# Block 1's expert sums on the matrix engine, gathers 25 places back, and a norm gain as columns

## The chip, the cores and the metric

The kernel runs on one core of a Trainium2 chip. The metric is the device time of one launch in microseconds, median of three runs. The engines are named as in the profile: PE multiplies matrices (its weight loads are listed apart as PEld), DVE is the vector engine, ACT the scalar engine, POOL issues the gathers (indirect DMAs), SP issues all other DMAs. Every engine, and each of the two DMA issuers, takes its instructions in the order that was fixed when the kernel was compiled.

## The reference, cut to what matters

One decoder layer over 1024 tokens of width 1024, all in fp32:

```python
h = x
h = h + hybrid_mixer(rms_norm(h, norm_mix), ...)          # convolution + delta rule, w_in, w_out
h = h + memory_cross_attention(rms_norm(h, norm_x), ...)  # 256 memory tokens, w_xq, w_xo
xn = rms_norm(h, norm_ffn)
# PEER: per token 8 heads x 16 best of 128*128 product keys = 128 experts
q = xn @ w_query; idx, gates = top16 of the sums of two top16 lists, softmax
act = gelu(einsum("td,ted->te", xn, expert_u[idx]))       # 128 dot products per token
y   = einsum("te,ted->td", gates * act, expert_v[idx])    # sum of 128 rows per token
out = rms_norm(h + y, norm_final)
```

`expert_u` and `expert_v` have 16384 rows of 1024. `rms_norm(h, norm_ffn)` is h times one number per token, times a gain per channel.

## The kernel before, in words

The tokens are eight blocks of 128. Three chunks go through mixer, attention and routing: `ca` (blocks 0, 1), `cb` (blocks 2 to 5, "the middle pass") and `cc` (blocks 6, 7).

The experts are done in two ways. Blocks 2 to 5 are done **densely**: `densify` builds on DVE, PE and ACT a table of gates per expert (`gd`), and `dense` multiplies these 512 tokens with all 16384 rows of both tables. Blocks 0, 1, 6 and 7 are **gathered**: for each of the 128 slots, POOL gathers one row of `expert_u` per token (a tile `g` of 512 KB, six buffers), and DVE forms the dot products in one instruction per slot (`gather_u`, L948). Then one row of `expert_v` per token is gathered. The sum over slots is made in one of two ways, by a bit of the constant `VD` for each block:

- `gather_v` with the bit set: one DVE instruction per slot adds gate times row to `y` (L1033);
- `gather_p` with the bit clear: the gathers run by token instead of by slot, the gates are spread out by DVE (L970), and PE makes four products for each pair of gathers (L984) in one PSUM bank `acc`. After 64 tokens ACT copies the bank (L996) to a short tile `t_s` (four buffers, also used by the routing), and SP takes it through DRAM (`yd`).

`VD` = 194 has bits 1, 6 and 7 set: only block 0 goes over PE. Both ways end in `finish`, which takes `g` buffers for h, for the final gain and, after `gather_p`, for y.

The order is written by hand. `merge` interleaves generators in proportion to their weights, and each `yield` is one step. `gathers(0)` has 518 steps: 3 of routing, 131 of `gather_u(0)` (with block 1's routing), 256 of `gather_u(1)` alternating with `gather_v(0)`, 128 of `gather_v(1)`. G1 to G4 = 98, 90, 107 and 17 of them stand beside the middle pass's projection, recurrence, attention and routing, G5 = 120 beside `tables2` (routing and `densify` of blocks 2 to 5) and the chunk `cc`; what is left stands beside `dense`, ahead of `gathers(6)`. `at` gives the steps of a generator another priority than their place: PG1 = 100 puts the first 295 steps (beside the middle pass) 100 places ahead, PG2 = -25 puts those beside G4 and G5 25 places behind. The tile scheduler then fixes the order of each engine by these priorities and its own estimate of when operands are ready.

`queries` normalises a chunk, writes the rows to DRAM (`xnd`) for `gather_u` and `dense`, and turns them to channels (`to_channels`). The gain `g_ffn` is applied to the rows there (L801), from a row that SP loads into all partitions (L796).

Of the kernel before, what the change touches and what calls it, by code (L numbers as in the profile page):

```python
# [9 lines left out]
F32 = mybir.dt.float32  # L10
# [6 lines left out]
OP = mybir.AluOpType  # L17
# [3 lines left out]
P = 128  # L21
SEQ = 1024
D = 1024
# [16 lines left out]
CSTART = [sum(CAND[:r]) for r in range(16)]  # L40
NCAND = sum(CAND)
NSLIP, CLOSE, PACE = 4, 3, 517
G1, G2, G3, G4, G5 = 98, 90, 107, 17, 120
A5 = -1
C4, T5 = 61, 92
NSHORT, NRAW, NHI, NLO, NG, LU, LV, VD = 6, 4, 2, 4, 6, 1, 1, 194
PG1, PG2, PG3, PT, PR, PD = 100, -25, 0, 0, 0, 0


def constants():  # L50
# [26 lines left out]
def merge(*gens):  # L77

    done = [0] * len(gens)
    live = [True] * len(gens)  # L80
    while any(live):
        j = min((i for i in range(len(gens)) if live[i]), key=lambda i: done[i] / gens[i][1])
        try:
            yield next(gens[j][0])
            done[j] += 1
        except StopIteration:
            live[j] = False


def run(*gens):  # L90
    for g in gens:
        for _ in g:
            pass
# [7 lines left out]
def steps(gen, n):  # L101
    for _ in range(n):
        if next(gen, 0) == 0:
            return
        yield
# [7 lines left out]
def _body(ctx, tc, I, out, dbg, front_only):  # L113
    nc = tc.nc
    act = nc.scalar.activation
    stt = nc.vector.scalar_tensor_tensor
    tt = nc.vector.tensor_tensor
    tsc = nc.vector.tensor_scalar
# [6 lines left out]
    gp = ctx.enter_context(tc.tile_pool(name="gp", bufs=NG))  # L125
# [3 lines left out]
    def dbgout(name, ap, idx):  # L129
        if name in dbg:  # L130
            nc.sync.dma_start(dbg[name][idx], ap)


    def unit():
        return qp.tile([P, 4, T], F32, name="unit")
# [9 lines left out]
    def psum():  # L145
        banks["n"] += 1
        return pp.tile([P, T], F32, name="ps" if banks["n"] % 2 or not banks["both"] else "po")
# [5 lines left out]
    def rows(n):  # L153

        r = []
        for _ in range((n + 1) // 2):
            v = unit().rearrange("p a t -> p (a t)")
            r += [v[:, 0:D], v[:, D:2 * D]]
        return r[:n]
# [29 lines left out]
    g_mix, g_x, g_mem, g_ffn = (cols[:, 8 * i:8 * i + 8] for i in range(4))  # L189
# [79 lines left out]
    def normalise(blocks):  # L269
        ss = sp.tile([P, NB], F32, name="ssn")  # L270
        rstd = sp.tile([P, NB], F32, name="rstdn")
        n = len(blocks)
        for b in range(n):
            sumsq(ss[:, b:b + 1], blocks[b])
        rsqrt(rstd[:, :n], ss[:, :n], 1.0 / D, EPS)
        return rstd
# [11 lines left out]
    def split_parts(nt=T):  # L288

        def one():  # L290
            if nt == T:
                return Parts([unit().bitcast(F32R) for _ in range(2)], 4)
            v = unit().bitcast(F32R).rearrange("p a t -> p (a t)")[:, :KD * nt]
            return Parts([v.rearrange("p (k t) -> p k t", k=KD)], KD)

        return one(), one()

    def to_channels(xhi, xlo, blocks, gain):

        nt = len(blocks) * P  # L300
        for k in range(KD):
            ps = psum()
            for b, x in enumerate(blocks):
                nc.tensor.transpose(ps[:, b * P:(b + 1) * P], x[:, k * P:(k + 1) * P], ident)
            if gain is None:
                act(xhi[:, k, :nt], ps[:, :nt], AF.Copy)
                tt(xlo[:, k, :nt], ps[:, :nt], xhi[:, k, :nt].bitcast(F32), op=OP.subtract)
            else:
                act(xhi[:, k, :nt], ps[:, :nt], AF.Copy, scale=gain[:, k:k + 1])
                stt(xlo[:, k, :nt], ps[:, :nt], gain[:, k:k + 1], xhi[:, k, :nt].bitcast(F32),  # L310
                    op0=OP.mult, op1=OP.subtract)

    def proj_ct(src, x, nt, key=None):

        xhi, xlo = x
        ps = psum()
        hi, lo = load_w(src, key)
        for k in range(KD):
            js = slice(k * P, (k + 1) * P)
            mm3(ps[:, :nt], hi[:, js], lo[:, js], xhi[:, k, :nt], xlo[:, k, :nt], k == 0, k == KD - 1)  # L320
            if k % 4 == 3:
                yield
        return ps[:, :nt]
# [466 lines left out]
    def queries(c):  # L790

        t0, NB, T = c.t0, c.nb, c.T
        hv = c.h
        rstd = normalise(hv)
        gffn = unit().rearrange("p a t -> p (a t)")[:, :D]
        nc.sync.dma_start(gffn, I["g_ffn_row"].partition_broadcast(P))  # L796
        xs = rows(NB)
        for b in range(NB):
            tb = slice(t0 + b * P, t0 + (b + 1) * P)
            nc.sync.dma_start(hd2[tb], hv[b])  # L800
            stt(xs[b], hv[b], rstd[:, b:b + 1], gffn, op0=OP.mult, op1=OP.mult)  # L801
            nc.sync.dma_start(xnd[tb], xs[b])
            dbgout("xn", xs[b], tb)
        x = split_parts(T)
        to_channels(x[0], x[1], xs, None)
        yield
        for b in range(NB):
            routes[c.b0 + b] = Route(c.b0 + b)
        for hh in range(4):
            pair = []  # L810
            keys = sp.tile([P, 2, P], F32, name="keys")
            nc.sync.dma_start(keys, I["keysT"][:, 2 * hh:2 * hh + 2])
            for i in (2 * hh, 2 * hh + 1):
                ps = yield from proj_ct(I["w_pq"][i], x, T, (c.keep, "w_pq", i))
                pair.append(short()[:, :T])
                act(pair[-1], ps, AF.Copy)
                yield
            for b in range(0, NB, 2):
                yield from best_keys(c.b0 + b, hh, pair, keys, b * P)
# [118 lines left out]
    def gather_u(r):  # L938

        tb = r.tb  # L940
        xn = gp.tile([P, D], F32, name="xn", bufs=1)
        nc.sync.dma_start(xn, xnd[tb * P:(tb + 1) * P])
        idx = r.a = gp.tile([P, NSLOT], F32, name="g_a", bufs=2)
        stt(idx, r.ki, 128.0, r.kj, op0=OP.mult, op1=OP.add)
        ii = r.ii = gp.tile([P, NSLOT], I32, name="g_ii", bufs=2)
        nc.vector.tensor_copy(ii, idx)
        for k, g in gathered("expert_u", ii, LU):
            stt(g, g, 1.0, xn, op0=OP.mult, op1=OP.mult, accum_out=r.a[:, k:k + 1])  # L948
            yield
# [131 lines left out]
    def dense(first):  # L1081

        xs = rows(NB)
        for b in range(NB):
            nc.sync.dma_start(xs[b], xnd[first + b * P:first + (b + 1) * P])
        x = split_parts()
        to_channels(x[0], x[1], xs, None)
        ev = I["expert_v"].rearrange("(i j) d -> j i d", j=P)
        y = []

# [50 lines left out]
        for b in range(NB):  # L1141
            tb = slice(first + b * P, first + (b + 1) * P)
# [69 lines left out]
    ga = at(pg, gathers(0))  # L1212
    tables2 = at("PT", tables(2))
# [5 lines left out]
    qb = queries(cb)  # L1219
    next(qb)  # L1220
    rest = at("PR", chain(inproj(cc), recurrence(cc), outproj(cc), cross(cc), queries(cc)))
    run(merge((steps(ga, G4), G4), (qb, 32), (steps(rest, C4), C4)))
    run(merge((steps(ga, G5), G5), (tables2, T5), (rest, 195 - C4)))

    pg['now'] = 'PG3'
    run(merge((chain(ga, at('PG3', gathers(6))), 1036 - G1 - G2 - G3 - G4 - G5), (at("PD", dense(2 * P)), PACE)))
# [52 lines left out]
```

## Time and profile before

| | |
|---|---|
| median of three runs | 3265.38 us (3265.27 to 3266.77) |
| the profiled execution | 3260.8 us, of which 3259.0 us is the span |
| PE, DVE, ACT, POOL busy | 86%, 78%, 41%, 40% of the span |
| mean granted TensorE clock | 0.913 of 2.4 GHz |
| DMA | 984.74 MB, 302 GB/s over the span |
| gathered | 1024 tiles of 512 KB: 536.94 MB |

In a row of a group of instructions, "busy, mean ns" is the time in which at least one of them ran and the mean of one; "idle before" is the time in which the engine stood still just ahead of them, with what ended most of it. In a row of stretches the columns are busy time and number of instructions of each engine, then the granted clock, the share of the DMA engines' time in use, and GB/s.

### The profile page before, as it was taken

The numbers are of one execution on the slowest core, as the hardware profiler recorded it, in microseconds if no ns is written. First come the engines' busy times: TensorE is split into PE (matmuls) and PEld (weight loads), VectorE is DVE, ScalarE is ACT, GpSimd is POOL, SyncE is SP. The second block draws the span as 40 slices with busy tenths as digits, with TensorE's granted clock in tenths as the row PEclk, the third lists the DMA queues.
The fourth block names the chain that finished last, engine by engine and source line by source line (L and its number), as shares of the span: only waits on it lengthen the run. The fifth ranks groups of instructions, "written<-read, shape, count | busy, mean of one in ns | idle before, by whom it ended". The sixth has DMA issues, their size and how long they took to land.

```text
span 3259.0 us, 42839 instructions
## 1 busy us (share of the span) xinstructions
PE 2786.7 (86%) x14826; PEld 2309.3 (71%) x14826; DVE 2550.9 (78%) x5311; ACT 1349.8 (41%) x2463; POOL 1319.0 (40%) x1028
## 2 busy tenths in 40 slices
PE   7897699847788898475665799999999999999997
PEld 7886588745554687364644687888888888888885
DVE  6654898797544588998887999887888888888874
ACT  5444343312222353334433354445444444454444
POOL 0000024475544332402453246555555655555530
PEclk9998789968989799687877899999999999999998
DMA  7555759898988998616999689999999999999983
GB/s 282 189 176 203 271 209 368 290 331 312 359 311 319 365 368 324 242 78 238 370 345 377 233 289 344 372 345 326 349 345 347 345 342 347 341 336 345 346 304 104
DMA packets 351417, 984.74 MB, mean 302 GB/s; under 512 B 30304, under 2 KB 99552, under 8 KB 347104
## 3 DMA queue, kind: packets, MB, share of 16 engines
q0 software_dynamic: 147456, 536.94, 44.9%
q1 hardware_dynamic: 203744, 445.08, 37.8%
q8 instruction: 116, 1.90, 0.2%
q14 instruction: 101, 0.83, 0.1%
HBM read 901.68 MB, written 80.22 MB: 301 GB/s over the span
## 4 chain that ended last, share of the span: by engine, by line
PE 44%; DVE 10%; DMA 3%; issue 2%; ACT 1%; POOL 0%; SPq 0%; DVEq 0%; ACTq 0%; POOLq 0%
PE ps L259 7%; PE ps L261 7%; PE ps L260 7%; PE po L261 7%; PE po L260 7%; PE po L259 7%; DVE unit L1066 1%; DVE g_y L1033 1%; DMA g<-expert_u,g_ii 1%; PE ps L1072 1%; DVE unit L1063 1%; DVE unit L1064 1%; DMA g<-expert_v,g_ii 1%; DMA wraw<-w_pq 1%; DMA unit<-g_ffn_row 1%
## 5 line engine op out<-in xcount | busy, mean ns | idle before, releaser
L931 POOL DMA_INDIRECT g<-expert_u,g_ii x512 | 636.7, 1244 | 1032.3 <-DVE t_s L833 443.5
L246 ACT ACTIVATE whi<-wraw 128x1024 fp32r<-128x1024 f32 x452 | 480.0, 1062 | 868.0 <-PE ps L260 481.7
L931 POOL DMA_INDIRECT g<-expert_v,g_ii x384 | 549.7, 1432 | 642.5 <-DVE g_y L1033 338.9
L948 DVE SCALAR_TENSOR_TENSOR g<-g,xn 128x1024 f32<-128x1024 f32 x512 | 618.0, 1218 | 165.0 <-DMA g<-expert_u,g_ii 155.7
L259 PE MATMUL ps<-unit,whi 128*128 128x512 f32 (+1 forms) x1784 | 655.5, 368 | 16.2 <-ACT whi L246 7.6
L261 PE MATMUL ps<-unit,wlo 128*128 128x512 f32 (+1 forms) x1784 | 648.5, 364 | 7.6 <-DMA wlo<-lod 4.9
L260 PE MATMUL ps<-unit,whi 128*128 128x512 f32 (+1 forms) x1784 | 649.1, 364 | 0.0
L252 DVE TENSOR_TENSOR wlo<-wraw,whi 128x1024 fp32r<-128x1024 f32 x332 | 406.4, 1225 | 293.5 <-ACT whi L246 284.9
L1033 DVE SCALAR_TENSOR_TENSOR g_y<-g,g_a,g_y 128x1024 f32<-128x1024 f32 x381 | 487.7, 1280 | 16.8 <-DMA g<-expert_v,g_ii 13.3
L260 PE MATMUL po<-wlo,unit 128*128 128x512 f32 x1136 | 442.8, 390 | 0.0
L261 PE MATMUL po<-whi,unit 128*128 128x512 f32 x1136 | 442.4, 389 | 0.0
L259 PEld LDWEIGHTS ps<-unit,whi 128*128 128x128 f32 x1784 | 348.8, 196 | 79.3 <-issue 11.5
L261 PEld LDWEIGHTS ps<-unit,wlo 128*128 128x128 f32 x1784 | 348.1, 195 | 60.0 <-DMA wlo<-lod 5.1
L259 PE MATMUL po<-whi,unit 128*128 128x512 f32 x1136 | 382.8, 391 | 1.9 <-ACT whi L246 1.9
L260 PEld LDWEIGHTS ps<-unit,whi 128*128 128x128 f32 x1784 | 348.8, 196 | 49.4 <-DVE unit L310 0.8
L259 PEld LDWEIGHTS po<-whi,unit 128*128 128x128 f32 x1136 | 213.2, 188 | 49.9 <-ACT whi L246 3.6
L260 PEld LDWEIGHTS po<-wlo,unit 128*128 128x128 f32 x1136 | 213.3, 188 | 46.6 <-issue 1.9
L261 PEld LDWEIGHTS po<-whi,unit 128*128 128x128 f32 x1136 | 213.4, 188 | 45.2 <-issue 0.8
L1126 ACT ACTIVATE unit<-po 128x512 f32<-128x512 f32 x256 | 152.7, 597 | 144.7 <-PE po L261 136.8
L977 POOL DMA_INDIRECT g<-expert_v,g_y x128 | 132.3, 1034 | 156.8 <-DVE g L948 53.3
L1113 ACT ACTIVATE po<-unit 128x512 f32<-128x512 f32 x248 | 144.4, 605 | 0.0
L1072 PE MATMUL ps<-unit 128*128 128x128 f16 x1024 | 86.6, 239 | 59.6 <-DVE unit L1066 47.7
(391 smaller groups left out, 4080.3 us busy)
## 6 DMA issues: line engine op xcount, KB each, us to landing
wraw<-u_t SPq DMA_DIRECT2D x128, 512.0 KB
wraw<-expert_v SPq DMA_DIRECT2D x128, 512.0 KB
wlo<-lod SPq DMA_DIRECT2D x120, 512.0 KB
wraw<-w_in SPq DMA_DIRECT2D x84, 512.0 KB
gd<-unit SPq DMA_DIRECT2D x32, 1024.0 KB
unit<-gd SPq DMA_DIRECT2D x32, 1024.0 KB
lod<-wlo SPq DMA_DIRECT2D x60, 512.0 KB
wraw<-w_out SPq DMA_DIRECT2D x24, 512.0 KB
```

Of the source, the lines that this page charges most:

```text
L246: act(hi, raw, AF.Copy)
L252: tt(lo, raw, hi.bitcast(F32), op=OP.subtract)
L259: nc.tensor.matmul(ps, lh, rh, start=first, stop=False, skip_group_check=open_)
L260: nc.tensor.matmul(ps, lh, rl, start=False, stop=False, skip_group_check=open_)
L261: nc.tensor.matmul(ps, ll, rh, start=False, stop=last, skip_group_check=open_)
L931: nc.gpsimd.indirect_dma_start(out=g, out_offset=None, in_=I[table], in_offset=bass.IndirectOffsetOnAxis(ap=ii[:, k:k + 1], axis=0))
L948: stt(g, g, 1.0, xn, op0=OP.mult, op1=OP.mult, accum_out=r.a[:, k:k + 1])
L977: nc.gpsimd.indirect_dma_start(out=g, out_offset=None, in_=I["expert_v"], in_offset=bass.IndirectOffsetOnAxis(ap=iT[:, t:t + 1], axis=0))
L1033: stt(y, g, a[:, k:k + 1], y, op0=OP.mult, op1=OP.add)
L1072: nc.tensor.matmul(ps[:, u * P:(u + 1) * P], part[i][:, g, :, t], oj[:, g, :, t], start=i == 0, stop=i == 1)
L1113: act(pss[b], y[b][:, half * 512:(half + 1) * 512], AF.Copy)
L1126: act(y[b][:, half * 512:(half + 1) * 512], pss[b], AF.Copy)
```

## The change

- `VD` becomes 192: block 1 goes through `gather_p` instead of the DVE sum.
- G5 becomes 206, and the weight of those steps 1.25 x 206: all 518 steps of `gathers(0)` now stand beside `tables2` and `cc` or earlier, and the last 206 are spread over the first four fifths of that stretch. Beside `dense` only `gathers(6)` is left.
- PG1 becomes -25: the gathers beside the middle pass stand 25 places behind their place instead of 100 ahead.
- `queries` no longer multiplies by the gain row and no longer loads it; `to_channels` applies the gain as a column per channel, in `queries` and in `dense`. The rows in `xnd` lack the gain, so `gather_u` loads the gain row into a `g` buffer for each block and multiplies `xn` by it.

```diff
-G1, G2, G3, G4, G5 = 98, 90, 107, 17, 120
+G1, G2, G3, G4, G5 = 98, 90, 107, 17, 206
-NSHORT, NRAW, NHI, NLO, NG, LU, LV, VD = 6, 4, 2, 4, 6, 1, 1, 194
-PG1, PG2, PG3, PT, PR, PD = 100, -25, 0, 0, 0, 0
+NSHORT, NRAW, NHI, NLO, NG, LU, LV, VD = 6, 4, 2, 4, 6, 1, 1, 192
+PG1, PG2, PG3, PT, PR, PD = -25, -25, 0, 0, 0, 0
@@ queries
-        gffn = unit().rearrange("p a t -> p (a t)")[:, :D]
-        nc.sync.dma_start(gffn, I["g_ffn_row"].partition_broadcast(P))
...
-            stt(xs[b], hv[b], rstd[:, b:b + 1], gffn, op0=OP.mult, op1=OP.mult)
+            tsc(xs[b], hv[b], rstd[:, b:b + 1], None, op0=OP.mult)
...
-        to_channels(x[0], x[1], xs, None)
+        to_channels(x[0], x[1], xs, g_ffn)
@@ gather_u
+        gffn = gp.tile([P, D], F32, name="g")
+        nc.sync.dma_start(gffn, I["g_ffn_row"].partition_broadcast(P))
+        tt(xn, xn, gffn, op=OP.mult)
@@ dense
-        to_channels(x[0], x[1], xs, None)
+        to_channels(x[0], x[1], xs, g_ffn)
@@ the order
-    run(merge((steps(ga, G5), G5), (tables2, T5), (rest, 195 - C4)))
+    run(merge((steps(ga, G5), 1.25 * G5), (tables2, T5), (rest, 195 - C4)))
```

## Rows read from the trace of the kernel before

**Rows 1.** The page: busy time of each engine, with its share of the span.

```profile
PE 2786.7 (86%) x14826; PEld 2309.3 (71%) x14826; DVE 2550.9 (78%) x5311; ACT 1349.8 (41%) x2463; POOL 1319.0 (40%) x1028
```

**Rows 2.** Busy time by stretch: length, PE, PEld, DVE, ACT, POOL, clock, DMA, GB/s.

```profile
444.00:600.00 156.00, 155.21 (x703) 128.94 (x702) 125.63 (x252) 71.58 (x127) 72.92 (x60) 0.97 0.97 370
600.00:800.00 200.00, 122.47 (x832) 105.70 (x832) 173.82 (x346) 45.10 (x123) 119.82 (x107) 0.79 0.86 303
800.00:1100.00 300.00, 246.27 (x1179) 166.43 (x1177) 152.59 (x338) 78.15 (x153) 139.60 (x134) 0.90 0.90 339
...
1300.00:1380.00 80.00, 40.65 (x283) 26.70 (x283) 72.80 (x192) 28.52 (x71) 34.27 (x27) 0.69 0.70 251
1380.00:1500.00 120.00, 72.03 (x615) 65.53 (x615) 112.72 (x335) 42.75 (x112) 0.23 (x1) 0.81 0.21 80
1500.00:1700.00 200.00, 133.59 (x954) 111.46 (x954) 180.35 (x293) 85.83 (x233) 104.28 (x66) 0.80 0.93 354
1700.00:1840.00 140.00, 84.89 (x573) 71.47 (x574) 116.60 (x377) 43.19 (x94) 38.61 (x29) 0.73 0.85 324
...
2000.00:3200.00 1200.00, 1197.69 (x5279) 989.85 (x5278) 988.41 (x1145) 575.59 (x832) 675.10 (x489) 1.00 0.94 339
```

**Rows 3.** L1033 alone by stretch: DVE busy, clock, DMA, GB/s.

```profile
1300.00:1500.00 200.00, 0.00 (x0) 0.76 0.41 148
1500.00:1840.00 340.00, 117.80 (x92) 0.77 0.90 342
1840.00:2000.00 160.00, 44.56 (x35) 0.99 0.86 294
```

**Rows 4.** Groups of instructions between 1300 and 1840 us.

```profile
L931 POOL DMA_INDIRECT g<-expert_v,g_ii x98 | 149.5, 1525 | 326.8 <-ACT unit L1076 120.5 <-DVE g_y L1033 105.8 <-DVE t_s L832 25.9
L1033 DVE SCALAR_TENSOR_TENSOR g_y<-g,g_a,g_y 128x1024 f32<-128x1024 f32 x92 | 117.8, 1280 | 10.5 <-DMA g<-expert_v,g_ii 9.3 <-issue 0.2
L1072 PE MATMUL ps<-unit 128*128 128x128 f16 x1024 | 86.6, 239 | 59.6 <-DVE unit L1066 47.7 <-ACT unit L1076 4.6 <-DVE unit L310 1.4
```

**Rows 5.** The chain of waits, 1300 to 1840 us: shares by line, one piece.

```profile
by line: DVE unit L1066 7.5%; issue 6.9%; DVE g_y L1033 5.9%; PE ps L1072 4.9%; DVE unit L1063 4.8%; DVE unit L1064 4.0%; PE ps L259 3.9%; DMA g<-expert_v,g_ii 3.8%; DMA wraw<-w_pq 3.5%; DMA unit<-g_ffn_row 3.5%; PE ps L260 3.4%; PE ps L261
...
1735.71 18.73 DMA unit<-g_ffn_row
```

**Rows 6.** Block 0's products: two PE groups, a weight-load group, 1300 to 1380 us.

```profile
L984 PE MATMUL ps<-g,g_y 128*32 128x512 f32 x256 | 42.1, 711 | 11.8 <-DMA g<-expert_v,g_y 11.8
L984 PE MATMUL po<-g,g_y 128*32 128x512 f32 x256 | 37.8, 665 | 24.8 <-DMA g<-expert_v,g_y 23.8 <-issue 0.9
L984 PEld LDWEIGHTS po<-g,g_y 128*32 128x32 f32 x256 | 5.2, 111 | 35.0 <-DMA g<-expert_v,g_y 19.8 <-DVE g L948 8.5 <-issue 6.2
L984 PE MATMUL ps<-g,g_y 128*32 128x512 f32 x64 | 12.4, 855 | 6.6 <-DMA g<-expert_v,g_y 6.6
```

**Rows 7.** PE in order of time: start, us, and the idle time before in brackets.

```profile
410.49 0.48 PE L304 MATMUL po<-call,unit 128*128 128x128 f32 x1 [23.83 <-DVE unit L421]
...
719.33 0.47 PE L695 MATMUL ps<-call,unit 128*128 128x128 f32 x1 [25.90 <-ACT unit L691]
```

**Rows 8.** DVE in order of time at 711 us, in the same columns.

```profile
710.95 1.23 DVE L948 SCALAR_TENSOR_TENSOR g<-g,xn 128x1024 f32<-128x1024 f32 x1 [1.22 <-DMA g<-expert_u,g_ii]
...
712.10 0.15 DVE L234 TENSOR_TENSOR rs_t<-rs_y 128x4 f32<-128x4 f32 x1
```

**Rows 9.** Who waited for whom: us in total, times, longest.

```profile
DVE g L948 <- DMA g<-expert_u,g_ii: 155.7, 73, 8.8
...
POOL g L931 <- ACT unit L1076: 120.5, 1, 120.5
```

**Rows 10.** Groups of instructions over the whole span.

```profile
L801 DVE SCALAR_TENSOR_TENSOR unit<-unit,rstdn 128x1024 f32<-128x1024 f32 x8 | 9.8, 1281 | 16.6 <-DMA unit<-g_ffn_row 16.5
...
L970 DVE TENSOR_TENSOR g_y<-g_y,masks 128x256 f32<-128x256 f32 x16 | 6.6, 416 | 2.0 <-PE po L984 1.1 <-ACT g_y L963 0.5 <-PE ps L984 0.4
...
L718 DVE TENSOR_SCALAR unit<-unit,rstdn 128x1024 f32<-128x1024 f32 x8 | 5.7, 769 | 0.1
```

More of the change, by code (lines that the diff above doesn't have):

```diff
@@ L800, in queries @@
             nc.sync.dma_start(hd2[tb], hv[b])
-            stt(xs[b], hv[b], rstd[:, b:b + 1], gffn, op0=OP.mult, op1=OP.mult)
+            tsc(xs[b], hv[b], rstd[:, b:b + 1], None, op0=OP.mult)
             nc.sync.dma_start(xnd[tb], xs[b])
-            dbgout("xn", xs[b], tb)
         x = split_parts(T)
-        to_channels(x[0], x[1], xs, None)
+        to_channels(x[0], x[1], xs, g_ffn)
         yield
```

## Prediction

> **What bounds the kernel now.** I read the page first, then a table of stretches, then the groups and the chain of waits in the stretch that the change touches most. PE is busy 86% of the span, DVE 78% [rows 1], but that is a mean over two regimes. From 2000 to 3200 us PE is busy 1197.69 of 1200 us at the full 2.4 GHz [rows 2]: this is the dense part. Its matmuls are not touched, so whatever leaves it (gathers, DVE sums) is worth nothing there; it only begins earlier or later. The kernel's time is therefore the moment at which the dense part has all it needs, near 1840 us, plus a fixed 1420 us.
>
> Before that PE has holes. In 600 to 800 us it is busy 122 of 200 us, in 800 to 1100 us 246 of 300, and from 1300 to 1840 us 331 of 540 (40.65 + 72.03 + 133.59 + 84.89), at a clock between 0.69 and 0.81 [rows 2]. DVE is the full engine where PE is empty: 174 of 200 us in 600 to 800, and 72.8 + 112.7 + 180.4 + 116.6 = 482 of the 540 us [rows 2]. DMA moves 339 to 370 GB/s in three of these stretches and only 80 GB/s from 1380 to 1500 us [rows 2]: there one wait of 120.5 us keeps POOL from gathering [rows 9]. So no engine is full for the whole of the first 1840 us; the order in which DVE serves the chunks and the gathers decides.
>
> **The change part by part.** I sum against the profiled execution, 3260.8 us, which is 4.6 us below the median of 3265.4; the 4.6 is added at the end.
>
> *Gathers 25 back instead of 100 ahead (444 to 1300 us).* Two waits show what 100 ahead costs. At 410 us PE stood for 23.8 us because the middle pass's normalised rows (L421) lay in DVE's queue behind block 0's routing. At 719 us it stood for 25.9 us on a copy that waited for a reciprocal root [rows 7], whose steps of 0.15 us each lay behind a gather's dot product of 1.23 us, some of which waited for their own DMA [rows 8]. Such waits for gathered rows are 155.7 us in all [rows 9]. With the gathers behind, the first wait goes almost whole (0 to -24, I take -20) and the second perhaps half (0 to -26, -13). What is late next: the gathers, by about what the chunk gains. The stretch already moves 303 to 370 GB/s, so a later start is not caught up for nothing; I charge 8 us (0 to 24, the whole of the first wait). Sum -25, between -50 and +24.
>
> *Block 1 over PE (1300 to 1840 us).* Removed: 127 DVE sums of 1.28 us, of which 92 (117.8 us) stand here, none of them before 1500 us, and 35 (44.6 us) after 1840, where they are worth nothing [rows 3]. So what they free lies between 1500 and 1840. On the chain of this stretch the sums hold 5.9% and the gathers that they wait for 3.8% of 540 us, 31.9 and 20.5 us [rows 5].
>
> Added: 256 products, 512 matmul records. Block 0's took 42.1 + 37.8 = 80 us, and at the low clock near 1340 us 12.4 us for 64 records, 99 us for 512 [rows 6]. I take 85. They wait in PE's queue for their gathers: block 0's PE waits were 11.8 + 24.8 us, and 8.5 more on the weight loads, 45 in all [rows 6]. Behind a waiting product stand the tables' matmuls and those of the last chunk, which the tables and the dense start wait for. How much of this 130 us is on the path? The nearest row is the tables' own PE work, 86.6 us busy [rows 4], 4.9% of 540 = 26.5 us on the chain [rows 5]: a share of 0.31. That gives +26 for the products and +14 for the waits, between 0 and +130. The 16 spreads of gates on DVE are 6.6 us [rows 10], at 0.3 on the path +2. The bank `acc` leaves three of four PSUM banks to tables and chunk; with four, PE waited 4.6 us for a bank to be copied out [rows 4]; I take +5, between 0 and 20.
>
> A check by engine: between 1500 and 1840 us DVE falls from 297 to about 186 us, PE rises from 218 to at most 303 of 340 [rows 2]. PE becomes the fuller engine there, and the stretch can shrink by 37 us at most, unless products move ahead of 1500, where PE is 113 of 200 us busy.
>
> *All of block 1 ahead of the dense part.* The 35 late gathers, 18 MB, come forward. The stretch moves 146 MB now (length times GB/s [rows 2]); 164 MB at the best rate shown, 370 GB/s, is 444 us. So they fit into 540 us if the hole is used: nothing charged here; if it stays shut they lengthen the other 420 us, which already run at 251 to 354 GB/s, by up to 18.3 MB at 354 GB/s = 52 us. `finish` of block 1 then holds three of six `g` buffers for some time, as block 0's did; the next gathers are those of `gathers(6)`, and there POOL is busy 675 of 1200 us [rows 2], which hides it.
>
> *The gain as columns.* The gain row leaves `queries`. Its load for the last chunk held the chain for 18.73 us [rows 5]; the multiplication falls from 1281 to 769 ns, eight times, 4 us in all [rows 10]. I take -18.7 (0 to -19): behind it stand the rows themselves and the weights, which came earlier. In its place four loads in `gather_u`, each on SP's queue waiting for a `g` buffer with weight loads behind it, and four multiplications of at most 1.28 us. A buffer turns over within 8.8 us, the longest wait for a gathered row [rows 9], so 0 to +9 for each of two blocks before the dense part; weights in four buffers hide most, I take +2 in all. The column form in `to_channels` is the one that the attention uses already: nothing.
>
> Sum of the stretch: -31.9 - 20.5 + 26 + 14 + 2 + 5 - 18.7 + 2 = -22. With the -25 of the middle pass -47: 3213.8 us profiled, and with 4.6 us **3218 us**.
>
> **A rule of the Trainium skill.** PE's clock was 0.69 where products waited beside tables (1300 to 1380 us) and 0.90 from 800 to 1100 us, where most of block 0's products ran, waits included [rows 2]. The Trainium skill, "TensorE: Matmul & The Clock Gate", section "HAM oscillation — how this bites in real kernels", says that bursts of matmuls with waits for DMA between them let the clock fall back each time. By it the products would slow what stands around them, and it is a rival below; the row of 800 to 1100 us bears it out only in part.
>
> **The rivals.**
>
> *The hole is filled (larger gain).* If block 1's products let gathers run from 1380 us on, the stretch is held by DMA alone: 164 MB at 354 GB/s is 464 us, -76, with the middle pass -101: 3164; at 370 GB/s 3144. For it: the products need no DVE sum to free a buffer, and the last 206 steps run at about twice the former pace. Against: the hole comes from block 0's `finish`, which is not changed, and PE's check allows only 37 us.
>
> *No difference.* The tables and the last chunk go on filling DVE, which was busy 185 of the 200 us before 1500 without one sum, and what the middle pass gains the late gathers lose: -6 to +6, about 3265.
>
> *Products block PE (slower).* One mechanism, between 1500 and 1840 us: the products wait in order, and the matmuls of `tables2` and `cc` behind them wait too. The price is 130 us times the share on the path. At 0.31 it is in my sum; from 0.68 it eats the whole gain ((40 + 47) / 130, about 0.67), at 0.9 it is 77 us more than I took: +30, 3295. For it: PE is already the engine that the check leaves fullest. Against: block 0's products cost PE a wait on DMA of only 37 us in 128 gathers.
>
> *The clock falls (slower).* All of PE's 331 us at a mean clock of 0.77 (the four clocks by their lengths [rows 2]) taken at 1.2 GHz are 510 us, with 99 of products 609: +69 on 540, less 25: about 3309. Stretches at 0.5 do not occur in the rows of this part, the lowest is 0.69.
>
> **How the numbers follow.** Forecast (3185 to 3250) 0.48; hole filled 0.14; no difference 0.12; products block 0.20; clock 0.06. Faster by over 0.2% (6.5 us, about what a measurement of this kernel can tell from no change): 0.48 + 0.14 = 0.62; within it 0.12; slower 0.20 + 0.06 = 0.26. The range leaves out the better half of the filled hole and the worse half of the two slow cases: 3150 to 3300, which also takes in the ends of the middle pass's term (-50, +24).
>
> **What would show it.** Right: no L1033 before the dense part and 512 more records of L984; PE's wait on L421 near 410 us gone, and fewer waits of DVE on `expert_u`; the load of the gain row no longer on the chain near 1736 us; the dense part's full PE beginning some 45 us before 1840 us; the dense part as long as before. Wrong: PE waits on `expert_v` well over 45 us for block 1, or PE waits on copies of the tables (L1076), with the dense part not earlier; the gathers still missing from 1380 to 1500 us and DMA full after it; or the middle pass ending no earlier than 1300 us because its gathers came later.

## The result, and the profile after

The changed kernel takes 3318.61 us (median of 4 runs, 3313.15 to 3319.95), the kernel before 3265.32 us beside it: ratio 1.0168, 95% interval 1.0142 to 1.0194. It is 53 us slower; 3218 was forecast, with 3150 to 3300 as the range. The profiled execution has a span of 3318.2 us.

First the page of the changed kernel, busy time of each engine (answers to [rows 1]):

```profile
PE 2894.8 (87%) x15340; PEld 2318.3 (70%) x15340; DVE 2409.4 (73%) x5206; ACT 1356.7 (41%) x2465; POOL 1264.2 (38%) x1028
```

The 512 added records of block 1's products are there (514 more in all); PE is busy 108 us longer, DVE 142 us shorter. The same stretches as in [rows 2], of the changed kernel:

```profile
444.00:600.00 156.00, 155.88 (x702) 129.57 (x701) 125.75 (x265) 71.98 (x128) 71.99 (x59) 0.96 0.96 368
600.00:800.00 200.00, 122.19 (x792) 105.40 (x791) 172.23 (x342) 44.82 (x121) 122.35 (x104) 0.76 0.84 299
800.00:1100.00 300.00, 263.89 (x1189) 168.07 (x1189) 146.14 (x331) 74.79 (x147) 133.67 (x133) 0.94 0.89 321
1300.00:1380.00 80.00, 43.66 (x286) 32.03 (x287) 73.06 (x251) 28.02 (x69) 31.18 (x29) 0.70 0.79 278
1380.00:1500.00 120.00, 71.88 (x574) 59.37 (x573) 119.11 (x350) 38.14 (x93) 9.01 (x7) 0.80 0.25 92
1500.00:1700.00 200.00, 144.50 (x977) 83.84 (x981) 89.54 (x197) 62.01 (x169) 73.29 (x73) 0.76 0.89 337
1700.00:1840.00 140.00, 115.68 (x820) 73.20 (x821) 68.61 (x141) 55.09 (x147) 52.95 (x49) 0.87 0.97 376
2000.00:3200.00 1200.00, 1198.08 (x5282) 990.77 (x5281) 985.06 (x1134) 576.90 (x833) 667.42 (x484) 1.00 0.94 336
```

The dense part is as it was. Between 1500 and 1840 us DVE falls from 297 to 158 us, more than the 186 us forecast, but in part because its work now lies later: up to the start of the dense part it falls from 311 to 232 us (rows below). Still the dense part begins later. Neither wait of [rows 7] is gone. PE of the changed kernel in order of time, idle time in brackets:

```profile
413.79 0.48 PE L304 MATMUL po<-call,unit 128*128 128x128 f32 x1 [22.50 <-DVE unit L421]
...
722.82 0.48 PE L695 MATMUL ps<-call,unit 128*128 128x128 f32 x1 [26.34 <-ACT unit L691]
```

**Where the time went.** I take the stretch from 1480 us, where the last chunk's recurrence runs, to the first multiplication of gates in the dense part. First the kernel before, columns as in [rows 2]:

```profile
1480.00:1840.00 360.00, 229.84 (x1635) 193.51 (x1636) 311.27 (x700) 137.01 (x351) 142.88 (x95) 0.77 0.86 329
```

Then the changed kernel, and its products (L984) alone in the same stretch (PE, weight loads, clock, DMA):

```profile
1480.00:1902.00 422.00, 315.66 (x2168) 200.50 (x2168) 231.57 (x704) 146.84 (x363) 132.78 (x128) 0.80 0.86 328
```

```profile
1480.00:1902.00 422.00, 93.95 (x512) 12.32 (x512) 0.80 0.86 328
```

The stretch is 62 us longer. PE spends 94 us on products, 222 instead of 230 on everything else, and is idle 106 us instead of 130. But 39.5 of the 106 us are new waits, right ahead of products, nearly all of them for the products' own gathers; the products' weight loads wait for gathers as well:

```profile
L984 PE MATMUL ps<-g,g_y 128*32 128x512 f32 x512 | 94.0, 737 | 39.5 <-DMA g<-expert_v,g_y 37.0 <-DVE unit L1063 2.5
PEld ps L984 <- DMA g<-expert_v,g_y: 54.1, 19, 8.2
```

So the products took up about half of PE's old idle time (130 us became 67), and brought 94 us of work and 39.5 us of standing.

The loss does not grow evenly. The last chunk's first state update comes at 1477 instead of 1461 us, so 16 of the 62 us had been lost before the stretch begins. Two steps of that chunk's attention (L749) show a jump, first of the kernel before, then of the changed one:

```profile
1599.08 0.46 ACT L749 ACTIVATE d_s<-ps,a_mx 128x256 f32<-128x256 f32 x1
1618.44 0.47 ACT L749 ACTIVATE d_s<-ps,a_mx 128x256 f32<-128x256 f32 x1 [6.41 <-DVE a_mx L746]
```

```profile
1630.23 0.48 ACT L749 ACTIVATE d_s<-ps,a_mx 128x256 f32<-128x256 f32 x1
1697.68 0.47 ACT L749 ACTIVATE d_s<-ps,a_mx 128x256 f32<-128x256 f32 x1 [2.78 <-DVE a_mx L746]
```

The first is 31 us late, the next 79. In between, from 1637 to 1682 us, PE does nothing but products and waits for their gathers, at a granted clock of 0.53, while DVE and ACT are busy for 1.3 and 0.5 of the 45 us. The stretch, and the chain of waits in it:

```profile
1637.00:1682.00 45.00, 23.98 (x104) 2.63 (x104) 1.27 (x3) 0.52 (x2) 24.34 (x26) 0.53 0.96 355
by line: DMA g<-expert_v,g_y 65.1%; PE ps L984 17.6%; issue 9.3%; POOL g L977 9.2%
```

Some 17 of the 79 us are won back before the dense part.

### The profile page after: what moved, and what is told of

Its sections match the earlier page's. It is cut to its first block, busy times and chain, and to the rows that moved or that the text cites. A ratio compares the mean times of both kernels' runs of the same rounds, so it can differ in the third digit from the quotient of the medians.

```text
span 3318.2 us, 43684 instructions
## 1 busy us (share of the span) xinstructions
PE 2894.8 (87%) x15340; PEld 2318.3 (70%) x15340; DVE 2409.4 (73%) x5206; ACT 1356.7 (41%) x2465; POOL 1264.2 (38%) x1028
## 4 chain that ended last, share of the span: by engine, by line
PE 45%; DVE 6%; DMA 4%; issue 3%; POOL 1%; ACT 1%; POOLq 0%; DVEq 0%; ACTq 0%
PE ps L259 7%; PE ps L261 7%; PE ps L260 7%; PE po L261 7%; PE po L260 7%; PE po L259 7%; DMA g<-expert_v,g_y 3%; PE ps L984 1%; PE ps L1072 1%; DVE g L948 1%; POOL g L928 1%; POOL g L977 1%; DMA g<-expert_u,g_ii 0%; DVE unit L1066 0%; DVE wlo L252 0%
## 5 line engine op out<-in xcount | busy, mean ns | idle before, releaser
L948 DVE SCALAR_TENSOR_TENSOR g<-g,xn 128x1024 f32<-128x1024 f32 x512 | 617.0, 1219 | 148.9 <-DMA g<-expert_u,g_ii 134.4
L928 POOL DMA_INDIRECT g<-expert_v,g_ii x256 | 357.5, 1396 | 271.2 <-DVE g_y L1033 199.5
L977 POOL DMA_INDIRECT g<-expert_v,g_y x256 | 263.7, 1030 | 507.1 <-PE ps L984 210.2
L259 PEld LDWEIGHTS ps<-unit,whi 128*128 128x128 f32 x1784 | 345.2, 194 | 77.9 <-ACT whi L246 11.3
L260 PEld LDWEIGHTS ps<-unit,whi 128*128 128x128 f32 x1784 | 344.4, 193 | 50.5 <-issue 1.7
L1033 DVE SCALAR_TENSOR_TENSOR g_y<-g,g_a,g_y 128x1024 f32<-128x1024 f32 x254 | 325.4, 1281 | 3.2 <-DMA g<-expert_v,g_ii 1.2
L984 PE MATMUL ps<-g,g_y 128*32 128x512 f32 x768 | 147.7, 727 | 63.8 <-DMA g<-expert_v,g_y 61.3
```

Of the source, the lines that this page charges most:

```text
L259: nc.tensor.matmul(ps, lh, rh, start=first, stop=False, skip_group_check=open_)
L260: nc.tensor.matmul(ps, lh, rl, start=False, stop=False, skip_group_check=open_)
L928: nc.gpsimd.indirect_dma_start(out=g, out_offset=None, in_=I[table], in_offset=bass.IndirectOffsetOnAxis(ap=ii[:, k:k + 1], axis=0))
L977: nc.gpsimd.indirect_dma_start(out=g, out_offset=None, in_=I["expert_v"], in_offset=bass.IndirectOffsetOnAxis(ap=iT[:, t:t + 1], axis=0))
L984: return nc.tensor.matmul(acc[32 * cc:32 * cc + 32], W[:, c, u], gs[c][:, half * 512:(half + 1) * 512], start=q == 0 and u == 0, stop=q == ...
L1033: stt(y, g, a[:, k:k + 1], y, op0=OP.mult, op1=OP.add)
```

## The experiments

"Before" in each comparison is the kernel before on the same chip, 3266 to 3269 us.

**The four parts of the change, one by one.** pg_only: `PG1 = -25` alone. gain_only: the edits of `queries`, `gather_u` and `dense` alone. order_only: G5 and its weight alone. pe_sums: those and VD = 192.

```diff
# pg_only
-PG1, ... = 100
+PG1, ... = -25
# order_only; pe_sums has the last two lines as well
-G5 = 120 ... (steps(ga, G5), G5)
+G5 = 206 ... (steps(ga, G5), 1.25 * G5)
-VD = 194
+VD = 192
```

> The kernel before with PG1 = -25 alone. In the changed kernel the middle pass is some 13 us later by the last chunk's projection (the first L421 of that chunk at 1127 instead of 1114 us). Theory: the priority does this, since the gathers start no sooner and are only served later; about 3277 us. Rival: the priority gains what was forecast (-25, about 3240) and the 13 us come from the gain loads that sit in gather buffers; a third way, that it moves nothing, is 3265.

> The kernel before with the gain as columns alone. Theory: the 18.7 us on the chain near 1736 us go, of which at least half is kept: 3246 to 3256 us. Rival: the loads of the gain row in gather buffers and on SP's queue cost as much or more, 3265 to 3280.

> The kernel before with G5 = 206 and weight 1.25 alone: block 1 keeps its DVE sums, all ahead of the dense part. If the place in the order is what costs (128 tiles of 512 KB to bring before the dense part), this is slower as well, by 20 to 50 us: 3285 to 3315. If the products on PE are what costs, this stays within 10 us of before, since DVE has the time from 1500 us on only in part: 3265 to 3275.

> The kernel before with block 1 over PE and its place in the order alone (VD = 192, G5 = 206, weight 1.25). Theory: this part alone costs what the stretch from 1410 us lost in the changed kernel, some 45 us: 3305 to 3315 us. Rival: without the other two edits the products would fall otherwise and the loss would be a joint one: under 3290.

Measured: pg_only 3283.97 us (1.0053, 1.0036 to 1.0070), gain_only 3246.96 (0.9931, 0.9905 to 0.9958), order_only 3287.99 (1.0073, 1.0049 to 1.0096), pe_sums 3323.09 (1.0168, 1.0151 to 1.0185); before 3268.07. So +16, -21, +20, and +35 for the products in the new order; the sum, +50, is the measured +53 within its error. The +35 is pe_sums less order_only: what products cost in the place of sums, all else in the order being equal. gain_only beats both kernels. The chain of waits of gain_only, 1300 to 1840 us, does not show the load of the gain row any more, where it held 3.5% [rows 5]:

```profile
by line: issue 9.7%; DMA wlo<-lod 6.2%; DVE unit L1066 5.3%; DMA wraw<-w_xo 4.3%; DMA wraw<-w_pq 4.1%; PE ps L1072 3.9%; DMA d_s<-kmd 3.8%; DMA unit<-xnd 3.2%; DVE unit L1063 2.7%; DVE g_y L1033 2.5%; PE ps L259 2.5%; DVE unit L1064 2.5%; D
```

**What PG1's +16 is.** In pg_only block 0's products have other matmuls among them. pg_solid keeps the four of a pair together by a priority 125 higher. That also puts the products, though not the gathers, back to the 100 places ahead that they had in the kernel before:

```diff
 PG1, ... = -25
+                    with tc.high_priority(offset=125):
                         with tc.issue_after(product(1, 0).ins):
```

> The kernel before with PG1 = -25 alone, as in pg_only (3284 us), and the four products of a pair of gathers kept together by a priority 125 higher, so that no other matmul stands between them. Theory 'broken groups' (with the gathers 25 behind, the products fall among the chunk's matmuls, two records by themselves take nearly as long as eight in a row, and block 0's products take 131 us instead of 87): the products take 85 to 95 us again and the time is 3262 to 3274 us, no difference from before. Rival 'late gathers' (the 16 us are the price of gathers that come later): the products take 85 to 95 us and the time stays at 3280 to 3288 us.

3268.38 us, ratio 1.0002 (0.9988 to 1.0016): no difference from before. So the later gathers by themselves cost nothing. The products alone, 740 to 1420 us, first of pg_only, then of pg_solid (79.85 us in the kernel before; the 131 and 87 us of the expectation take in the waits within each group of products):

```profile
740.00:1420.00 680.00, 100.60 (x512) 13.70 (x512) 0.87 0.86 312
```

```profile
740.00:1420.00 680.00, 78.25 (x512) 11.03 (x512) 0.87 0.86 314
```

PE in order of time, pg_only, two pairs of gathers:

```profile
1051.28 1.05 PE L984 MATMUL ps<-g,g_y 128*32 128x512 f32 x2
1052.68 1.06 PE L984 MATMUL ps<-g,g_y 128*32 128x512 f32 x6
...
1070.82 1.05 PE L984 MATMUL ps<-g,g_y 128*32 128x512 f32 x2
1072.46 1.04 PE L984 MATMUL ps<-g,g_y 128*32 128x512 f32 x2
1073.87 1.04 PE L984 MATMUL ps<-g,g_y 128*32 128x512 f32 x2
1075.27 1.04 PE L984 MATMUL ps<-g,g_y 128*32 128x512 f32 x2
```

and pg_solid, one pair:

```profile
1082.23 1.06 PE L984 MATMUL ps<-g,g_y 128*32 128x512 f32 x8
```

Two records take as long as eight. A pair whose four products stand apart costs 4.2 us of PE instead of 1.06. But most of these 22 us lie before 1120 us, and there pg_only is not behind pg_solid: DVE makes the last normalised rows of the last chunk (L421) at 1125.9 us in pg_only and at 1126.9 us in pg_solid. What differs after that is how long PE stands ahead of products for their gathers, 1120 to 1420 us, first pg_only, then pg_solid:

```profile
L984 PE MATMUL ps<-g,g_y 128*32 128x512 f32 x184 | 33.7, 730 | 26.4 <-DMA g<-expert_v,g_y 26.4
L984 PE MATMUL ps<-g,g_y 128*32 128x512 f32 x176 | 28.8, 691 | 8.8 <-DMA g<-expert_v,g_y 8.8
```

So the +16 comes from the products' place in PE's order. Whether through torn groups or through these 18 us of waits is not shown, since pg_solid took away both; the times point to the waits.

**Less work in the products, or fewer bytes.** half_products leaves one of four products of block 1 in 30 of each 32 pairs; half_rows gathers 512 of each 1024 numbers of block 1's rows of `expert_v` and multiplies them twice. The sum of block 1 is another one in both.

```diff
# half_products
+                    if r.tb == 1 and 0 < 4 * q + u < 31:
+                        product(1, 0)
+                    else:
# half_rows
-  out=g, in_=I["expert_v"]
+  out=g[:, :512], in_=I["expert_v"].rearrange("e (h d) -> (e h) d", h=2)
```

> The changed kernel with one product of four left for block 1 (30 of its 32 pairs in each half; three quarters of the sum are left out), all gathers as they were: some 70 of the 94 us of PE's product time go, its waits for gathers stay. Theory of PE's time: the kernel falls by 30 us or more, under 3290. Theory of waits in PE's order, and theory of DMA: at most 10 us, 3308 to 3320.

> The changed kernel with block 1's expert_v gathers of half a row (512 numbers of other rows; the sums are not those of the reference), 33.5 MB less, as many gathers and products. Theory of DMA (the hole from 1410 to 1480 us stays shut and 128 tiles must pass after it at 330 to 360 GB/s): the loss goes, 33.5 MB at 350 GB/s is up to 95 us, under 3275. Theory of PE's time: no change, 3310 to 3320. Theory of waits: in between, since each wait for a gather is shorter.

3313.41 us (1.0144, 1.0108 to 1.0181) and 3322.86 us (1.0163, 1.0122 to 1.0204): neither gains. That does not clear PE's time of the loss. The products of half_products alone:

```profile
1480.00:1896.00 416.00, 81.71 (x152) 10.06 (x152) 0.84 0.87 335
```

152 records still hold PE for 82 us, against 94 us for 512: what was left out had run beside what was kept. The run did not take away what it was to take away. In half_rows the order on PE moved too (product 97 stood behind 560 instead of 640 matmuls of the tables), so skip_rows repeats it with the order kept up to product 129: rows with a number over 8191, about half, are left out of block 1's gathers.

```diff
+  bounds_check=8191, oob_is_err=False      # block 1's gathers of expert_v
```

> The changed kernel, but block 1's gathers of expert_v leave out the rows with a number over 8191, about half of them, so block 1's sum is formed in part of what lay in the buffer. The order on PE is that of the changed kernel up to product 129, with at most 3% more matmuls ahead of the later ones. Theory 'DMA is full': 33 MB less at 350 GB/s are up to 95 us of transfers; the stretch is then held by something else, about as in the kernel before, and the dense part begins 35 to 60 us earlier, 3260 to 3285 us. Rival 'waiting in lockstep' (each gather's time from issue to landing counts, not its bytes): 3305 to 3320 us, as half_rows.

3313.13 us (1.0132, 1.0114 to 1.0150), 5 us less than the changed kernel and within the error. The stretch of skip_rows:

```profile
1480.00:1901.00 421.00, 314.68 (x2203) 202.11 (x2203) 239.78 (x765) 150.65 (x379) 158.88 (x128) 0.83 0.72 258
```

DMA falls to 258 GB/s, and length and PE stay. In this order the bytes are not what counts. The time from a gather's issue to its landing may still be: PE's waits ahead of products are 30.6 us there.

**What stands behind the products.** Four edits of the changed kernel: hole makes block 1's indices in `gather_u` so that its gathers can start before block 0's end; lead puts the products behind the next pair of gathers; act_stores lets ACT issue the stores to `yd`; solid_act has these stores and the groups kept together.

```diff
# hole
-            st = slip()
+            st = short()[:, :T]        # and block 1's iT made in gather_u
# lead
-  with tc.issue_after(product(1, 0).ins): ...
+  late.append(products)
+  if len(late) > 1: late.pop(0)()
# act_stores
-                nc.sync.dma_start(yd[...], st[32 * c:32 * c + 32])
+                nc.scalar.dma_start(yd[...], st[32 * c:32 * c + 32])
```

> The changed kernel with the gather hole opened: block 1's transposed indices are made at the start of its gather_u instead of behind the routing on DVE, and the bank of sums is copied to a short tile of the chunk pool instead of one that the routing holds. Theory of DMA: gathers run from 1410 us on, the 18 MB more find room, the kernel falls by 30 to 50 us, 3270 to 3290. Theory of waits: the same number of products wait in PE's order, only sooner; less than 15 us, 3303 to 3318.

> The changed kernel with the four products of a pair of gathers placed behind the next pair (for blocks 0 and 1), the same work and bytes. Theory of waits in PE's order: PE waits for gathers (37 us of products' waits after 1410 us) fall to under 15 and the kernel by 20 to 40 us, 3280 to 3300. Theory of DMA: no change, 3312 to 3322, since the gathers come no sooner. It could even be slower: each pair holds its buffers longer.

> The changed kernel with the stores of the product sums to yd (L999) issued by ACT instead of SP; nothing else differs. Theory 'SP stands behind a store' (SP waits at L999 for the copy L996 after the last product of a half, 46 us in two waits between 1500 and 1900 us, with the loads of the last chunk's attention behind it): the dense part begins 30 to 45 us earlier, 3275 to 3290 us. Rival 'DVE and PE are held by the gates and products themselves': SP's wait goes to L1079 or to a load, and the time stays at 3310 to 3325 us.

> The changed kernel with both edits, the four products of a pair kept together and the stores to yd issued by ACT. If 'broken groups' and 'SP stands behind a store' both hold and add up: 3255 to 3275 us. If only the first holds: 3295 to 3310 us; only the second: 3275 to 3290 us; neither: 3310 to 3325 us.

hole 3320.85 us (1.0161, 1.0132 to 1.0190), lead 3339.68 (1.0211, 1.0190 to 1.0232), act_stores 3328.90 (1.0178, 1.0154 to 1.0203), solid_act 3325.15 (1.0169, 1.0147 to 1.0191). None helps, and lead is 21 us slower than the changed kernel. solid_act failed for its first half too: the products fell only from 94 to 85 us there. gain_act, the stores by ACT in gain_only, was the same as gain_only:

> The kernel before with the gain as columns alone, as in gain_only (3247 us), and the stores to yd issued by ACT. Here only block 0 goes over products, in the middle pass. Theory 'SP stands behind a store': if the store holds loads of the middle pass too, 3230 to 3243 us. Rival: block 0's products end well ahead of the loads, so nothing waits there, 3243 to 3252 us.

3245.78 us (0.9937, 0.9914 to 0.9960).

**Where the products stand and what they wait for.** The place from 1637 to 1682 us, where ACT and DVE both stand behind products that wait for gathers, looks like this. ACT:

```profile
1682.39 0.60 ACT L996 ACTIVATE t_s<-ps 128x512 f32<-128x512 f32 x1 [44.87 <-PE ps L984]
```

DVE, same time:

```profile
1656.95 0.42 DVE L970 TENSOR_TENSOR g_y<-g_y,masks 128x256 f32<-128x256 f32 x1 [18.36 <-PE ps L984]
1669.45 0.42 DVE L970 TENSOR_TENSOR g_y<-g_y,masks 128x256 f32<-128x256 f32 x1 [12.08 <-PE ps L984]
1682.39 0.42 DVE L970 TENSOR_TENSOR g_y<-g_y,masks 128x256 f32<-128x256 f32 x1 [12.51 <-PE ps L984]
```

no_wait lets block 1's products read that block's normalised rows instead of the gathered ones, which are gathered for nothing. late100 spreads the changed kernel's 206 steps over the whole stretch. vd_only is the kernel before with VD = 192.

```diff
# no_wait
-  gs[c][:, half * 512:(half + 1) * 512]
+  (r.xn if r.tb == 1 else gs[c])[:, half * 512:(half + 1) * 512]
# late100
-  1.25 * G5
+  1.0 * G5
```

> The changed kernel, but block 1's products read that block's normalised rows, which lie in SBUF, instead of the gathered rows of expert_v; the rows are still gathered, and nothing waits for them. So block 1's sum is formed of other numbers. Theory 'all engines stand for the gathers' (in the changed kernel's order the products stand in a row on PE where the gathers are behind, ACT's copy L996 and DVE's spreads L970 wait behind them, 45 us from 1637 us on): the attention of the last chunk takes 80 to 90 us again instead of 134, the dense part begins 40 to 60 us earlier, 3255 to 3280 us. Rival 'the products' own work, spreads and copies' : 3300 to 3320 us.

> The changed kernel with the weight of the 206 steps 1.0 instead of 1.25, so that they spread over the whole stretch beside tables2 and cc: in PE's order the products then stand evenly among the tables' and the attention's matmuls (products 97 to 129 no longer in a row), and the last quarter after the tables. Theory 'all engines stand for the gathers': the stop of 45 us goes, the time is 3270 to 3300 us. Rival 'each product waits for its gather wherever it stands' : the waits are spread over more places, and the time stays at 3305 to 3325 us.

> The kernel before with VD = 192 alone: block 1 goes over products, with G5 = 120 and its weight as before. In PE's order the first of block 1's products then stands behind the attention of the last chunk, and most of them beside the dense part. Theory 'all engines stand for the gathers': nothing stops between 1500 and 1750 us, but what PE spends and waits on products beside the dense part, where it has no idle time, is added whole: 3265 to 3300 us, with the dense part longer by the products' time, some 40 to 60 us, and its start earlier by 10 to 30. Rival 'products are dear wherever they stand': as pe_sums, 3310 to 3330 us, with a late start of the dense part.

no_wait 3348.74 us (1.0243, 1.0206 to 1.0280), late100 3314.75 (1.0138, 1.0101 to 1.0176), vd_only 3318.74 (1.0159, 1.0129 to 1.0190). The theory that the stop of 45 us is the whole cost falls: in late100 ACT waits no longer than 14.6 us at a time, and the dense part begins at 1872 instead of 1902 us, but it takes 20 us longer, 15 of them products that now stand in it, and in all 4 us are won, within the error. no_wait is no clean test: PE was idle for 160 us of that stretch, perhaps because its gathers, which no product held back any more, went ahead of the chunk's loads. vd_only is the clearest. Its two stretches, before the dense part and the dense part:

```profile
1480.00:1822.00 342.00, 246.48 (x1854) 185.58 (x1855) 210.24 (x621) 137.88 (x353) 62.00 (x62) 0.85 0.78 297
1822.00:3234.00 1412.00, 1407.21 (x6269) 1126.03 (x6268) 1063.35 (x1406) 661.58 (x949) 748.16 (x548) 1.00 0.91 323
```

and its products alone in them:

```profile
1480.00:1822.00 342.00, 35.74 (x224) 5.20 (x224) 0.85 0.78 297
1822.00:3234.00 1412.00, 42.51 (x288) 6.19 (x288) 1.00 0.91 323
```

The kernel before, for comparison:

```profile
1840.00:3204.00 1364.00, 1356.89 (x5965) 1119.45 (x5964) 1144.65 (x1461) 660.98 (x948) 748.81 (x542) 1.00 0.94 333
```

The dense part takes 1412 us instead of 1364: 48 us more, 42.5 of them products. The gathers of vd_only also end later than its dense part (last sum of a slot near 3299 us), which sets its time. Over all runs with these parts (us, from 1480 to the start of the dense part; then the gathers issued in it, and the dense part's own length):

| | length | products on PE | rest of PE | PE idle | gathers | dense part |
|---|---|---|---|---|---|---|
| before | 360 | 0 | 230 | 130 | 95 | 1364 |
| order_only | 372 | 0 | 227 | 145 | 107 | 1371 |
| vd_only | 342 | 36 | 211 | 95 | 62 | 1412 |
| late100 | 392 | 64 | 224 | 103 | 106 | 1383 |
| half_products | 416 | 82 | 216 | 118 | 128 | 1361 |
| skip_rows | 421 | 91 | 223 | 106 | 128 | 1361 |
| half_rows | 422 | 90 | 220 | 111 | 125 | 1368 |
| after | 422 | 94 | 222 | 106 | 128 | 1363 |
| hole | 423 | 88 | 217 | 118 | 122 | 1363 |
| solid_act | 426 | 85 | 221 | 120 | 125 | 1364 |
| act_stores | 430 | 97 | 220 | 113 | 128 | 1362 |
| pe_sums | 432 | 95 | 214 | 124 | 125 | 1363 |
| lead | 446 | 95 | 218 | 133 | 128 | 1362 |
| no_wait | 463 | 64 | 239 | 160 | 128 | 1356 |

Less what PE spends on products, the stretch takes 306 to 351 us wherever there are products, but for no_wait (399), and 360 and 372 us where there are none. That fits a price in PE's time, but does not prove it: where fewer products stand in the stretch (vd_only, late100), fewer gathers do too, and half_products, with 12 us less of products and as many gathers, is only 6 us shorter.

**The load on DMA by itself.** extra_load adds to the kernel before 16 copies of 1 MB within DRAM behind the stores of the tables, as many bytes as 32 gathers; nothing reads them. gain_g90 is gain_only with G5 = 90, so that fewer gathers stand ahead of the dense part.

```diff
# extra_load, in densify
+  nc.sync.dma_start(junk[4 * n + q - 8, ...], gd[4 * n + q - 2, ...])
# gain_g90
-G5 = 120
+G5 = 90
```

> The kernel before with 16 additional copies of 1 MB within DRAM (16.8 MB, as much as 32 gathers), issued by SP between 1590 and 1840 us behind the stores of the tables' gates (L1079); nothing reads them. Theory 'DMA is full': 16.8 MB at 350 GB/s, +35 to +50 us on the start of the dense part, 3300 to 3316 us. Rival 'DMA has room, what costs is the products in order': +0 to +12 us, 3266 to 3278.

> The kernel before with the gain as columns (gain_only, 3247 us) and G5 = 90 instead of 120: up to 30 gathers and sums of block 1 fewer ahead of the dense part, and more beside it. Theory 'each gather ahead of the dense part costs 0.9 to 1.3 us': 3212 to 3225 us, as long as the dense part hides them. Rival 'the dense part's DMA (0.94 busy) and DVE are full': the dense part gets longer by as much, 3240 to 3260 us.

extra_load 3303.78 us (1.0092, 1.0064 to 1.0121): +36, with not one product more. Its stretches:

```profile
1500.00:1600.00 100.00, 70.04 (x542) 59.73 (x541) 91.14 (x170) 48.16 (x128) 41.70 (x24) 0.81 0.95 370
1600.00:1700.00 100.00, 52.53 (x390) 45.02 (x389) 67.35 (x105) 30.46 (x90) 35.40 (x24) 0.73 1.01 387
1700.00:1840.00 140.00, 80.15 (x562) 67.68 (x563) 106.34 (x237) 45.10 (x107) 53.68 (x42) 0.73 0.97 379
```

So in the order of the kernel before DMA had little room either. Part of the +36 may be the queue and not the bytes: SP, which issues the copies (L1082) in order with the chunk's loads, waited for the stores that they read.

```profile
SPq L1082 <- DMA gd<-unit: 50.2, 8, 16.0
```

No run parts the two. order_only agrees with the bytes: it has 107 gathers instead of 95 between 1480 us and the dense part, 6.3 MB more; at extra_load's 36 us for 16.8 MB that is 13 us, and its stretch grew by 12.

gain_g90 3301.69 us (1.0100, 1.0081 to 1.0118), worse, but not as the rival said. The dense part begins at 1806 instead of 1832 us (gain_only) and takes 11 us less. What is late is the gathered blocks: POOL gathers nothing from 1500 to 1700 us, and at the end, 3160 to 3300 us, PE has run dry while gathers still run.

```profile
1500.00:1600.00 100.00, 68.16 (x520) 58.38 (x520) 66.54 (x137) 45.46 (x120) 0.00 (x0) 0.81 0.64 236
1600.00:1700.00 100.00, 68.49 (x495) 57.24 (x493) 49.25 (x100) 42.09 (x120) 0.00 (x0) 0.83 0.54 196
...
3160.00:3300.00 140.00, 32.19 (x142) 25.97 (x140) 120.45 (x157) 22.23 (x37) 88.07 (x71) 0.63 0.86 315
```

## Why the prediction was wrong

*The products and their waits at a share of 0.31 of the path, against 52 us given back by DVE's sums: this is the step that failed.* The size was right: 130 us were put at work and waits, and PE spends 94 us on the products and stands 39.5 us ahead of them. The share was not. In the sum, block 1 over PE came to -5 us (-31.9 - 20.5 + 26 + 14 + 2 + 5); measured, pe_sums less order_only, it is +35. The 0.31 was the share of the tables' own matmuls on the chain, and a product that waits for its gather in PE's queue holds more than its own work: from 1637 to 1682 us the chunk's attention and the tables stood still with it, on a chain that is 65.1% gathers on their way and 17.6% products, and between the two steps of the attention around that place 48 us were lost. My check by engine let PE fill 303 of 340 us; it filled 260. The sign of being wrong that I had named, waits on `expert_v` well over 45 us, came: 37.0 us ahead of products and 54.1 ahead of their weight loads. The rival "products block PE" had the mechanism, with 3295 us at a share of 0.9 and a chance of 0.20.

What of this is PE's time and what is waiting for gathers stays open. Beside the dense part vd_only shows PE's time as the price: 42.5 of 48 us, with PE busy for 1407 of 1412. For the stretch before it no run settles it: where all products of block 1 were kept there, no edit made them shorter by more than 10%, but for no_wait, which lost more elsewhere; and no run took the waits away without other harm.

*The sums on DVE, -52.* DVE did fall, from 311 to 232 us in the stretch, but the stretch grew. The share of a line on the chain of waits is not what its removal gives.

*The middle pass, -25.* It costs +16. The steps "the first wait goes almost whole" and "the second perhaps half" failed: both waits are there, 22.50 and 26.34 us. What failed is that the new priority would clear DVE's queue there. It did not: in both kernels 14 dot products of gathers (L948) stand between the first and the last step of the reciprocal root ahead of the second wait, and ahead of the first wait 17.1 us pass in both from the first step of such a root to L421, full of the routing's searches. More than half of these (on 128x128 scores) belong to `queries`, which PG1 does not move. DVE of the changed kernel, ahead of the second wait:

```profile
717.04 1.22 DVE L948 SCALAR_TENSOR_TENSOR g<-g,xn 128x1024 f32<-128x1024 f32 x1
718.19 0.16 DVE L236 SCALAR_TENSOR_TENSOR rs_y<-rs_t,rs_y 128x4 f32<-128x4 f32 x1
718.29 1.22 DVE L948 SCALAR_TENSOR_TENSOR g<-g,xn 128x1024 f32<-128x1024 f32 x1
```

So the cause that the prediction named for the two waits was not taken away, and is neither confirmed nor refuted. The cost came from where I had looked for none, the products' place in PE's order.

*The gathers that come forward, charged at nothing.* order_only measured +20, between the 0 that I took and the 52 that I had kept for the range. DMA's 0.93 and 0.85 in [rows 2] hinted at it.

*The gain as columns, -18.7 + 2.* Right: -21.

*The dense part as long as before, the spreads of gates at 6.6 us.* Right: 1363 us, and 6.7 us busy. But DVE waited 94.1 us ahead of these spreads, for products that free a buffer, which the 6.6 us left out; no run took that wait away by itself.

*The clock.* Over the stretch it rose from 0.77 to 0.80, so that rival is out as a whole. Where products follow waits it bites: from 1637 to 1682 us the granted clock is 0.53, close to the lower level of 1.2 GHz, eight records take 1.93 us in the row below (changed kernel, PE in order of time) and 1.06 us in the row of pg_solid, and PE's clock was 0.76 from 1500 to 1700 us, where it had been 0.80 [rows 2]. By the rule weighed in the prediction (the Trainium skill, "TensorE: Matmul & The Clock Gate", section "HAM oscillation — how this bites in real kernels") the whole stretch should have slowed; these rows bear it out for the products that wait, not for the stretch.

```profile
1649.02 1.93 PE L984 MATMUL ps<-g,g_y 128*32 128x512 f32 x8 [6.43 <-DMA g<-expert_v,g_y]
```

## What to carry to other kernels

Idle time of an in-order engine that comes from a chain of dependencies is not free room: charge work that is moved onto such an engine in full, with its own waits and with what stands behind them, less only what a row shows to fit. Here 134 us of work and waits took up 63 us of idle time. Take a change with four parts apart first; here one part was worth -21 us and three cost 16, 20 and 35, and what a part costs can lie in its neighbours (a place in the order that tears products apart or lets them wait). When a priority is changed, read in the trace whether the order changed at the place that was meant. Before an experiment counts as "half of the work", read in its trace how long the engine was busy with it.

## What the hardware showed that I had not expected

- Four products with 32 columns each, eight records, take 1.06 us when they stand together, and two records take 1.04 us by themselves: a group torn into four costs 4.2 us. With three of four products left out in nearly all pairs, PE saved 12 of 94 us. The Trainium skill, "TensorE: Matmul & The Clock Gate", section "Part 3: Packing small matmuls — row/col tiling", says that products in different column groups run at the same time; the rows agree for products that stand together, and show none of the gain where one other matmul stands between them.
- 16.8 MB more, in a stretch whose DMA share was 0.93 and 0.85, cost 36 us in one order of PE (waits in SP's queue included), while 32 MB less gained 5 us, within the error, in another.
